# A planned two-layer diffusion step on one core: three conditioning maps go from TensorE to VectorE, and the planner gets a port model and priorities by part

## The chip, the core and the metric

One core of one Trainium2 chip runs the whole kernel. TensorE (PE) multiplies, VectorE (DVE), ScalarE (ACT) and GpSimd (POOL) do the elementwise work, and SyncE (SP) issues every DMA from one queue, in order. The metric is the device time of one execution in microseconds. The kernel before took a median of 1888.9 us in 3 runs (1887.55 to 1890.82).

## The reference, cut to what matters

Two layers work on 384 tokens (128 of context, 256 of a latent grid) of width 1024. Each layer is a half-step FFN, a mixer and a second half-step FFN:

```python
m = (jax.nn.silu(cond) @ lp['ada_w'] + lp['ada_b']).reshape(cond.shape[0], 1, N_MOD, D_MODEL)
x = x + 0.5 * mod(2) * swiglu(modulate(x, lp['norm_w'][0], mod(0), mod(1)), ...)
y, st = mixer(modulate(x, lp['norm_w'][1], mod(3), mod(4)), lp, *mixer_args)
x = x + mod(5) * y
x = x + 0.5 * mod(8) * swiglu(modulate(x, lp['norm_w'][2], mod(6), mod(7)), ...)
```

A conditioning map `(l, m)` is one of the nine slices of `ada_w` of layer `l`: a 1024 x 1024 matrix times two conditioning vectors. Its 4 MB are used once. Maps 1, 4 and 7 scale and 0, 3 and 6 shift the input of the three parts of a layer; 2, 5 and 8 are the gates of their outputs. The mixer projects the input to 23 tiles and runs three sub-mixers on them: an RWKV-7 recurrence, attention, and a gated DeltaNet. Both recurrences are computed in chunks, for which many small triangular matrices are inverted.

## The kernel before, in words

**Products.** Weights are fp32. Each 128-column tile comes by DMA (`wr`), ACT rounds it to fp32r (`whi`), DVE takes the rest (`wlo`), and `mm3` issues three matmuls for each block of 128 rows. An FFN makes 22 pairs of tiles, `pg` and `pu` (24 matmuls each), then 8 tiles `po` (66 matmuls each). DVE and ACT turn a pair into one tile `h`. The norm's factor `rstd` comes from one product `rps`, after the first pairs have been started.

**Conditioning maps.** `SIDE` has one string for each of the six stages (FFN, mixer, FFN of layer 0, the same of layer 1), and its letters give the maps that the stage computes, in the order of `l` and `m` from map 2 of layer 0 on. A letter `v` puts the map on DVE (line 874 on): 8 DMAs of 512 KB (`arow`), and for each two `tensor_tensor_reduce` over 1024 columns against a broadcast vector (`crow`), each followed by a short read of the sum into `mods`. A letter `m` puts it on TensorE: 8 DMAs of 512 KB (`araw`), 16 matmuls of 512 columns into `aps`, a copy `ev`, a way through DRAM (`adas`) and a small product. The kernel before has `"mmm"` for the mixer of layer 0: map 7 and map 8 of layer 0 and map 0 of layer 1.

**Inversion.** `stage_inv` runs twice in a mixer. It inverts 32 x 32 blocks in 31 steps, each of one product `pr` and one subtraction into `Z`, strictly one after the other. Each of the 62 instructions may go to DVE or to POOL.

**What sets the order.** Nothing is issued where it is written. A `Recorder` notes every operation with what it reads and writes, and `order()` plans the whole program: it walks through a modelled time, and each engine takes the waiting operation of the highest priority, which is its longest path to the end plus `BIAS` of its part (`label`). `estimate` gives each operation's planned cost. Where an operation may go to several engines (`op.alts`), the one that would finish it first takes it. On TensorE, `near` says how much less important an operation may be and still go ahead of one that needs another array shape. Where the plan sees TensorE without enough work, it puts in dummy matmuls (`idle_ps`, a 128 x 128 bf16 product that nobody reads), so that the clock stays up; they are fixed instructions of the program. `issue` then emits the plan: nearly all instructions have its line 718, table loads 714 and dummies 706.

Of the kernel before, what the change touches and what calls it, by code (L numbers as in the profile page):

```python
# [33 lines left out]
SHUF = [(j + 16) % 32 for j in range(32)]  # L34


SIDE = ("vvvvv", "mmm", "vvvv", "vvvv", "", "")

ROOM = {"kA": "h", "kS": "h", "vt": "h", "pt": "h", "ev": "h", "w0b": "h", "lora": "h", "yb": "r"}
TUNE = {'near': 2000.0, 'ahead': 8000.0, 'ahead2': 8000.0, 'finish': 5000.0, 'clock': True, 'dummy': 53.5, 'd1': 3600.0, 'd2': 7000.0}  # L40

BIAS = {'ada02': -100000.0, 'ada03': -100000.0, 'ada04': -100000.0, 'ada05': -100000.0, 'ada06': -100000.0, 'ada07': 0.0, 'ada08': 0.0, 'ada10': 0.0, 'ada11': -100000.0, 'ada12': -100000.0, 'ada13': -100000.0, 'ada14': -100000.0, 'ada15': -100000.0, 'ada16': -100000.0, 'ada17': -100000.0, 'ada18': -100000.0}
PLACES = {"u": 30, "r": 3, "w": 6, "a": 3, "b": 2, "h": 5, "t": 10, "ps": 7, "mxs": 2, "dram_ada": 2, "dram_s1": 2, "dram_s2": 2, "dram_s3": 2, "s4": 6}


# [123 lines left out]
class Op:  # L169
    __slots__ = ("eng", "meth", "args", "kw", "cost", "lat", "preds", "succs", "bufs", "idx", "cp", "need", "ready",  # L170
                 "start", "end", "tset", "label", "group", "seed", "filler", "follows", "pos", "held", "stall", "dma", "alts", "done",
                 "name", "real", "parts", "seq", "lead", "mode", "out")


class _Eng:
# [22 lines left out]
class Recorder:  # L198
# [91 lines left out]
    def any(self, *choices):  # L290

        op = self.add(*choices[0][:2], (), choices[0][2])
        op.alts = {}
        for eng, meth, kw in choices:
            op.eng, op.meth, op.kw = eng, meth, kw
            self.estimate(op)
            op.alts[eng] = (meth, kw, op.cost, op.lat, op.tset)
        self.choose(op, min(op.alts, key=lambda e: op.alts[e][2]))
        return op

    def choose(self, op, e):
        op.eng = e
        op.meth, op.kw, op.cost, op.lat, op.tset = op.alts[e]

    def copy(self, out, in_, pool=True):
        c = [("scalar", "copy", dict(out=out, in_=in_)), ("vector", "tensor_copy", dict(out=out, in_=in_))]
# [69 lines left out]
    def estimate(self, op):  # L376
# [4 lines left out]
        views = [v for v in list(a) + list(kw.values()) if isinstance(v, View)]  # L381
        ps = any(v.buf.tag in PSUM for v in views)
        sc = sum(isinstance(kw.get(k), View) for k in ("scalar", "scalar1", "scalar2", "bias", "scale", "accum_out"))
        op.tset, op.dma = None, 0.0
        e, m = op.eng, op.meth
        if m == "dma_start":
            nbytes = n * out.shape[0] * 4
            run = min(v.shape[-1] for v in (out, kw["in_"])) * 4
# [2 lines left out]
        elif e == "tensor":  # L391
            op.lat = 200.0
            op.seq = [self.product(*p) for p in op.parts]
            op.held = sum(p[3] for p in op.seq)
            op.cost = self.stream(0.0, op.seq, [0.0] * 16, 1.0)[1]
            op.mode, op.out = op.seq[0][4], op.seq[-1][4]
        elif e == "vector":
            if m == "tensor_reduce":
                n = int(np.prod(kw["in_"].shape[1:]))
            if m == "reciprocal":  # L400
                n *= 6
            full = ps or m in ("stream_shuffle", "tensor_reduce", "reciprocal") or any(k in kw for k in ("in1", "data"))
            op.cost = (65 + (n if full else n / 2)) / 0.96 + 62 * sc
            if m == "memset":
                op.cost = 8 + n
            op.lat = 130.0
        elif e == "scalar":
            op.cost = ((61 if isinstance(kw["in_"], View) and kw["in_"].buf.tag in PSUM else 112) + n) / 1.2 + 93 * sc
            op.tset = TSETS.get(kw.get("func"))
            op.lat = 142.0  # L410
        else:
            op.cost = 130 + n * (4.3 if sc else 3.3)
            if m == "memset":
                op.cost = 35 + n * 0.83
            elif m == "tensor_tensor":
                op.cost = 150 + n * 2.1
            elif m == "scalar_tensor_tensor":
                op.cost = 95 + n * 1.39
            op.lat = 120.0

    def wait(self, op, o):
        if op.eng == "tensor" and o.eng == "tensor":
# [3 lines left out]
    def order(self):  # L426
# [79 lines left out]
        def enter(op):  # L506
# [4 lines left out]
            else:  # L511
                heapq.heappush(gated, (op.pos - (self.ahead2 if op.follows else self.ahead), op.idx))

        win, busy, over, warm, ndum, past, dens, colt = 0, 0.0, 0.0, False, 0, [], 0.0, [0.0] * 16
        mode, nsw = (P, P), 0
        bus, tset, now, out, emit, wake, stuck = 0.0, None, 0.0, [], [], [], False
        for op in ops:
            if op.need == 0:
                enter(op)
        while len(out) < len(ops):  # L520
# [10 lines left out]
            for e in engs:  # L531
# [6 lines left out]
                while avail[e]:  # L538
# [15 lines left out]
                        op.stall = tag  # L554
                        continue
                    if op.alts:
                        here, best = now + op.alts[e][2], 1e18
                        for f in op.alts:
                            if f != e:
                                queue = sum(ops[x[1]].cost for x in avail[f] if x < item and not ops[x[1]].done)  # L560
                                best = min(best, max(free[f], now) + queue + op.alts[f][2])
# [89 lines left out]
                if op.tset and op.tset != tset:  # L651
                    tset = op.tset
                    cost += 1300.0
                op.start = now
                free[e] = now + cost
                if e != "tensor":
# [1249 lines left out]
```

## Time and profile before

| | us |
|---|---|
| median of 3 runs | 1888.9 |
| the profiled execution | 1892.28 |
| its span, first to last instruction | 1890.5 |
| FFN 1 of layer 0: pairs, then `po` | 184.45 + 92.48 |
| mixer of layer 0 | 360.08 |
| FFN 2 of layer 0 | 191.44 + 92.26 |
| FFN 1 of layer 1 | 191.11 + 92.31 |
| mixer of layer 1 | 349.36 |
| FFN 2 of layer 1 | 189.57 + 92.58 |

The stages were cut where the first matmul of the next one starts in the chain of work that ended last. A mixer includes its output product. Busy times are shown by stage in the section of rows below; in the mixers those of TensorE hold the dummies too, which have rows of their own.

### The profile page before, as it was taken

To read this page: it belongs to the slowest core of one execution; us is meant where nothing else is said; L and a number is where in the kernel's file an instruction comes from. 1 tells how busy PE (TensorE), PEld (TensorE's weight loads), DVE (VectorE), ACT (ScalarE), POOL (GpSimd) and SP (SyncE) were. 2 spreads that over 40 slices of the span, in tenths; PEclk is the share of its full clock that TensorE was granted. 3 is DMA by queue.
4 is the path that set the end of the run, shared out by engine and by line. 5 is a ranking of instruction groups with operands and counts; after the bars stand their busy time and mean duration, and the time that the engine had idled before them with its cause. 6 is when DMAs were issued, how large, how long until landed. Compare 5 with 4: busy or idle time off the path is not lost.

```text
span 1890.5 us, 34461 instructions
## 1 busy us (share of the span) xinstructions
PE 1842.2 (97%) x13589; PEld 1690.1 (89%) x13589; DVE 1336.9 (71%) x2680; ACT 856.4 (45%) x1777; POOL 206.2 (11%) x322
## 2 busy tenths in 40 slices
PE   8999999989999999999999999998899999999998
PEld 6999999778766799999999999997686679999998
DVE  3999954886775679995459995458879646555444
ACT  4444433657445454443344443347664444434323
POOL 0000000251320200000000000014525011000000
PEclk9999999999899999999999999999999999999999
DMA  9566644365421255664455664443341213434442
GB/s 363 200 222 230 241 137 164 124 196 157 109 46 39 78 205 203 216 241 126 125 201 206 214 243 126 126 137 91 79 102 42 66 52 101 123 123 123 128 123 84
DMA packets 144033, 279.46 MB, mean 148 GB/s; under 512 B 50192, under 2 KB 76880, under 8 KB 143872
## 3 DMA queue, kind: packets, MB, share of 16 engines
q1 hardware_dynamic: 143872, 277.26, 46.1%
q8 instruction: 107, 1.75, 0.4%
q14 instruction: 54, 0.44, 0.1%
HBM read 264.80 MB, written 11.89 MB: 146 GB/s over the span
## 4 chain that ended last, share of the span: by engine, by line
PE 82%; DVE 8%; ACT 4%; POOL 2%; DMA 2%; issue 1%; SPq 0%; DVEq 0%; ACTq 0%; POOLq 0%
PE po L718 23%; PE pg L718 20%; PE pu L718 20%; PE pw L718 5%; PE idle_ps L706 3%; POOL pr L718 1%; ACT L714 1%; POOL Z L718 1%; PE q L718 1%; PE z L718 1%; DVE mxs L718 1%; PE gram L718 1%; PE pr L718 1%; PE aps L718 1%; PE sc L718 1%
## 5 line engine op out<-in xcount | busy, mean ns | idle before, releaser
L718 DVE TENSOR_TENSOR wlo<-wr,whi 128x1024 fp32r<-128x1024 f32 (+2 forms) x334 | 400.8, 1203 | 90.4 <-ACT whi L718 90.1
L718 ACT CAST whi<-wr 128x1024 fp32r<-128x1024 f32 (+2 forms) x334 | 339.7, 1019 | 174.4 <-PE po L718 84.4
L718 PE MATMUL pg<-xs,whi 128*128 128x386 f32 x1408 | 366.3, 341 | 0.2 <-POOL xs L718 0.2
L718 PE MATMUL pu<-xs,whi 128*128 128x386 f32 x1408 | 365.8, 341 | 0.0
L718 PE MATMUL po<-h,whi 128*128 128x384 f32 x1408 | 360.1, 337 | 0.0
L718 PEld LDWEIGHTS pg<-xs,whi 128*128 128x128 f32 x1408 | 257.4, 189 | 0.9 <-POOL xs L718 0.5
L718 PEld LDWEIGHTS pu<-xs,whi 128*128 128x128 f32 x1408 | 257.4, 189 | 0.0
L718 DVE CUSTOM_DVE_ANT_0 unread<-arow,crow 128x1024 bf16<-128x1024 f32 x208 | 253.8, 1220 | 3.0 <-ACT crow L718 1.1
L718 PEld LDWEIGHTS po<-h,whi 128*128 128x128 f32 x1408 | 255.7, 188 | 0.0
L718 PE MATMUL pu<-xs,wlo 128*128 128x386 f32 x704 | 238.8, 339 | 0.6 <-DVE wlo L718 0.6
L718 PE MATMUL pg<-xs,wlo 128*128 128x386 f32 x704 | 238.7, 339 | 0.0
L718 PE MATMUL po<-h,wlo 128*128 128x384 f32 x704 | 237.4, 337 | 0.0
L718 PE MATMUL pw<-xs,whi 128*128 128x386 f32 (+1 forms) x736 | 198.4, 350 | 9.8 <-ACT whi L718 7.1
L718 DVE SCALAR_TENSOR_TENSOR xT<-po,mods,xT 128x256 f32<-128x256 f32 (+1 forms) x96 | 35.3, 413 | 169.4 <-PE po L718 169.2
L718 PEld LDWEIGHTS pw<-xs,whi 128*128 128x128 f32 (+1 forms) x736 | 131.7, 186 | 21.3 <-ACT whi L718 8.6
L718 PE MATMUL pw<-xs,wlo 128*128 128x386 f32 (+1 forms) x368 | 128.4, 350 | 7.8 <-DVE wlo L718 7.6
L718 PEld LDWEIGHTS pu<-xs,wlo 128*128 128x128 f32 x704 | 134.1, 190 | 1.1 <-DVE wlo L718 1.1
L718 PEld LDWEIGHTS pg<-xs,wlo 128*128 128x128 f32 x704 | 134.1, 190 | 0.5 <-DVE wlo L718 0.4
L718 PEld LDWEIGHTS po<-h,wlo 128*128 128x128 f32 x704 | 132.1, 188 | 0.0
L706 PEld LDWEIGHTS <-idle_z 128*128 128x128 bf16 x1553 | 96.1, 100 | 33.2 <-issue 26.6
L706 PE MATMUL idle_ps<-idle_z 128*128 128x128 bf16 x1553 | 123.4, 224 | 0.0
L718 ACT CAST h<-up 128x384 fp32r<-128x384 f32 x88 | 45.2, 514 | 151.0 <-DVE up L718 151.0
(363 smaller groups left out, 2466.1 us busy)
## 6 DMA issues: line engine op xcount, KB each, us to landing
wr<-in_ffn_in SPq DMA_DIRECT2D x176, 512.0 KB, 4.5
arow<-in_adat SPq DMA_DIRECT2D x104, 512.0 KB, 3.6
wr<-in_ffn_out SPq DMA_DIRECT2D x64, 512.0 KB, 3.7
wr<-in_w_in SPq DMA_DIRECT2D x44, 512.0 KB, 4.5
wr<-in_ffn_out SPq DMA_DIRECT2D x32, 384.0 KB, 3.3
araw<-in_ada SPq DMA_DIRECT2D x24, 512.0 KB, 5.2
araw<-in_ada SPq DMA_DIRECT2D x32, 256.0 KB, 6.5
wr<-in_w_out SPq DMA_DIRECT2D x16, 512.0 KB, 4.0
```

Of the source, the lines that this page charges most:

```text
L706: self.nc.tensor.matmul(ps[:, 0:n], lhsT=z[:, 0:P], rhs=z, start=True, stop=True)
L714: self.nc.scalar.preload_act_table_set(cur)
L718: ins = getattr(getattr(self.nc, op.eng), meth)(*[fix(x) for x in args], **{k: fix(x) for k, x in kw.items()})
```

## The change

It has four parts. `SIDE` puts the three maps of the first mixer on DVE, so that the six stages compute 6, 0, 5, 4, 0 and 1 maps on DVE instead of 5, 0, 4, 4, 0 and 0, and none on TensorE. The planner gets a model of the SBUF port that DVE and POOL share (`turn`, `op.port`): an operation of one that needs it waits in the plan until the other's is over, and the choice of engine counts that. Some planned costs change, those of POOL mostly upward. `near` goes from 2000 to -1, so that TensorE always takes the operation of the highest priority, and `BIAS` gets 23 entries for parts of the two mixers.

```diff
-SIDE = ("vvvvv", "mmm", "vvvv", "vvvv", "", "")
+SIDE = ("vvvvvv", "", "vvvvv", "vvvv", "", "v")
-TUNE = {'near': 2000.0, 'ahead': 8000.0, ...
+TUNE = {'near': -1.0, 'ahead': 8000.0, ...
+    "attn2.1": 22600.0, "gates.0": 12700.0, "inv0.0": -16400.0, "inv0.1": -22600.0, "inv1.1": -9500.0,
...
-            op.cost = 130 + n * (4.3 if sc else 3.3)
+            op.cost = 480 + n * (4.3 if sc else 3.3)
...
+        if e == "vector" and not ps and m not in ("stream_shuffle", "reciprocal", "tensor_reduce", "memset"):
+            op.port = 2 if src == 2 else 3
+        elif e == "gpsimd":
+            op.port = 1 if m == "memset" else 2
...
+        def turn(e, kind, t):
+            x = port["gpsimd" if e == "vector" else "vector"] if kind else (0.0, 0.0)
+            if kind == 1:
+                return max(t, x[1])
+            return max(t, x[0], x[1] if kind == 3 else 0.0)
...
-                        here, best = now + op.alts[e][2], 1e18
+                        here, best = turn(e, op.alts[e][5], now) + op.alts[e][2], 1e18
...
+                if op.port:
+                    cost += turn(e, op.port, now) - now
```

**TensorE, start of the first mixer.** `pw` is a projection, `aps` a conditioning map, `xs` the scaled input. Before:

```order
L718 MATMUL po_3066<-h_2423,wlo_3124 128x384
L718 MATMUL pw_3174<-xs_2408,whi_3162 128x386 x2
L718 MATMUL aps_3177<-araw_3103,cond_68 32x512 x2
L718 MATMUL aps_3177<-araw_3110,cond_68 32x512 x2
L718 MATMUL pw_3174<-xs_2408,wlo_3170 128x386
L718 MATMUL pw_3174<-xs_2528,whi_3162 128x386 x2
```

and now:

```order
L750 MATMUL po_3107<-h_2422,wlo_3161 128x384
L750 MATMUL pw_3209<-xs_2428,whi_3182 128x386 x2
L750 MATMUL pw_3209<-xs_2428,wlo_3192 128x386
L750 MATMUL pw_3209<-xs_2537,whi_3182 128x386 x2
L750 MATMUL pw_3209<-xs_2537,wlo_3192 128x386
```

The 48 products `aps` of the first mixer (two passes each) and the three small products behind them are gone. The dummies between the mixers' first `pw` and last `po` product go from 552 to 537 in layer 0 and from 595 to 468 in layer 1.

**POOL, second half of the first inversion in the mixer of layer 1.** `R` is the matrix, `pr` and `Z` the two halves of a step, and the size tells the step. Before:

```order
L718 TENSOR_TENSOR pr_13825<-R_13469,Z_13482 112x231
L718 TENSOR_TENSOR Z_13482<-Z_13482,pr_13825 112x21x11
L718 TENSOR_TENSOR pr_13825<-R_13469,Z_13482 112x240
L718 TENSOR_TENSOR Z_13482<-Z_13482,pr_13825 112x20x12
L718 TENSOR_TENSOR pr_13825<-R_13469,Z_13482 112x247
L718 TENSOR_TENSOR Z_13482<-Z_13482,pr_13825 112x19x13
L718 TENSOR_TENSOR pr_13825<-R_13469,Z_13482 112x252
L718 TENSOR_TENSOR pr_13825<-R_13469,Z_13482 112x255
```

and now:

```order
L750 TENSOR_TENSOR pr_13853<-R_13418,Z_13430 112x192
L750 TENSOR_TENSOR Z_13430<-Z_13430,pr_13853 112x24x8
L750 TENSOR_TENSOR Z_13430<-Z_13430,pr_13853 112x22x10
L750 TENSOR_TENSOR pr_13853<-R_13418,Z_13430 112x247
L750 TENSOR_TENSOR Z_13430<-Z_13430,pr_13853 112x18x14
L750 TENSOR_TENSOR Z_13430<-Z_13430,pr_13853 112x17x15
L750 TENSOR_TENSOR pr_13853<-R_13418,Z_13430 112x252
```

Most of the steps that POOL had are on DVE now. Of the 248 instructions `pr` and `Z` of the four inversions POOL had 107 and has 60; DVE goes from 141 to 188.

**DVE, start of the last FFN.** `gt` and `up` are the first work on the pairs, and an `ISA` row is a `tensor_tensor_reduce` of a map, or the read of its sum. Before:

```order
L718 TENSOR_TENSOR wlo_17680<-wr_17644,whi_17670 128x1024
L718 TENSOR_TENSOR wlo_17713<-wr_17676,whi_17703 128x1024
L718 TENSOR_TENSOR wlo_17747<-wr_17709,whi_17733 128x1024
L718 TENSOR_TENSOR gt_17766<-pg_17527,rstd_17743 128x384
L718 TENSOR_TENSOR gt_17771<-pg_17600,rstd_17743 128x384
L718 TENSOR_TENSOR up_17777<-pu_17567,rstd_17743 128x384
```

and now:

```order
L750 ISA unread_17503,mods_15_8193<-arow_17456,crow_17435 128x1024
L750 ISA mods_15_8193 128x1
L750 TENSOR_TENSOR wlo_17562<-wr_17474,whi_17537 128x1024
L750 ISA unread_17503,mods_15_8193<-arow_17456,crow_17442 128x1024
L750 ISA mods_15_8193 128x1
L750 ISA unread_17503,mods_15_8193<-arow_17523,crow_17435 128x1024
L750 ISA mods_15_8193 128x1
L750 TENSOR_TENSOR gt_17607<-pg_17347,rstd_17553 128x384
```

The last FFN now begins with a map, as the two FFNs in the middle did before. The dummies after `rps` go from 42 to 61, from 42 to 54 and from 19 to 54 in the last three FFNs.

## Rows read from the trace of the kernel before

**Rows 1.** The page's busy times of TensorE and its chain by line

```profile
PE 1842.2 (97%) x13589; PEld 1690.1 (89%) x13589; DVE 1336.9 (71%) x2680; ACT 856.4 (45%) x1777; POOL 206.2 (11%) x322
...
PE po L718 23%; PE pg L718 20%; PE pu L718 20%; PE pw L718 5%; PE idle_ps L706 3%; POOL pr L718 1%; ACT L714 1%; POOL Z L718 1%; PE q L718 1%; PE z L718 1%; DVE mxs L718 1%; PE gram L718 1%; PE pr L718 1%; PE aps L718 1%; PE sc L718 1%
```

**Rows 2.** Windows by stage: start:end, length, busy us of each engine, clock, DMA

```profile
41.72:226.17 184.45, 183.82 (x1056) 182.54 (x1056) 175.83 (x297) 81.20 (x157) 0.00 (x0) 1.00 0.66 227
226.17:318.65 92.48, 92.48 (x529) 92.48 (x529) 51.67 (x97) 30.95 (x48) 1.92 (x22) 1.00 0.48 150
318.65:678.73 360.08, 342.82 (x3387) 268.55 (x3387) 261.74 (x655) 195.57 (x458) 90.33 (x120) 0.97 0.39 112
678.73:870.17 191.44, 191.44 (x1102) 190.67 (x1102) 172.92 (x289) 84.66 (x162) 1.30 (x1) 1.00 0.62 214
1245.85:1595.21 349.36, 330.10 (x3329) 267.73 (x3328) 256.32 (x625) 189.68 (x450) 102.38 (x160) 0.98 0.30 80
1595.21:1784.78 189.57, 189.57 (x1079) 189.06 (x1078) 101.37 (x154) 79.93 (x158) 1.30 (x1) 1.00 0.40 122
```

**Rows 3.** Windows of the dummies alone, tile `idle_ps`: length, PE busy, clock, DMA

```profile
318.65:678.73 360.08, 47.87 (x552) 0.97 0.39 112
...
1245.85:1595.21 349.36, 48.41 (x595) 0.98 0.30 80
```

**Rows 4.** Lines of TensorE in the first mixer: busy us, mean ns, idle before

```profile
L718 PE MATMUL aps<-araw,cond 128*32 128x512 f32 x96 | 14.3, 672 | 0.0
```

**Rows 5.** Waits of the DMA queue in the first mixer: us, times, longest

```profile
SPq L718 <- DVE wlo L718: 65.2, 17, 14.2
SPq L718 <- PE aps L718: 62.2, 9, 23.1
```

**Rows 6.** The chain that ended last, 440 to 470 us: start, us, what

```profile
446.98 7.75 DMA wr<-in_w_in
```

**Rows 7.** Timeline of TensorE at the start of the second FFN

```profile
700.58 1.00 PE L706 MATMUL idle_ps<-idle_z 128*128 128x128 bf16 x15
...
701.83 1.68 PE L706 MATMUL idle_ps<-idle_z 128*128 128x128 bf16 x27
```

**Rows 8.** Tile `pr` on POOL in layer 1: ns min/median/max

```profile
L718 POOL TENSOR_TENSOR pr<-R,Z x36: 239/577/2102, 1317.6 to 1460.0; 112x60 f32<-112x60 f32 x4, 112x87 f32<-112x87 f32 x4, 112x31 f32<-112x31 f32 x3, 112x207 f32<-112x207 f32 x3
```

**Rows 9.** Tile `pr` on DVE in layer 0

```profile
L718 DVE TENSOR_TENSOR pr<-R,Z x42: 191/346/1114, 399.6 to 539.9; 112x156 f32<-112x156 f32 x4, 112x192 f32<-112x192 f32 x4, 112x240 f32<-112x240 f32 x4, 112x175 f32<-112x175 f32 x3
```

**Rows 10.** Timeline of POOL, 1330 to 1336 us, in the same inversion

```profile
1331.17 0.60 POOL L718 TENSOR_TENSOR pr<-R,Z 112x220 f32<-112x220 f32 x1
1332.27 2.06 POOL L718 TENSOR_TENSOR pr<-R,Z 112x231 f32<-112x231 f32 x1 [0.50 <-DVE Z L718]
```

**Rows 11.** Timeline of DVE, the same stretch

```profile
1332.64 1.22 DVE L718 TENSOR_TENSOR wlo<-wr,whi 128x1024 fp32r<-128x1024 f32 x1
1333.77 1.89 DVE L718 SCALAR_TENSOR_TENSOR cv<-prj,vecs,cv 128x386 f32<-128x386 f32 x2
```

**Rows 12.** Waits in the mixer of layer 1, 1287 to 1390 us

```profile
DVE Z L718 <- POOL pr L718: 6.8, 4, 2.6
POOL pr L718 <- DVE Z L718: 6.6, 8, 2.7
```

**Rows 13.** Timeline of DVE in the third FFN, with a map beside it

```profile
1030.66 0.55 DVE L718 TENSOR_TENSOR gt<-pg,rstd 128x384 f32<-128x384 f32 x1
1031.13 1.22 DVE L718 TENSOR_TENSOR wlo<-wr,whi 128x1024 fp32r<-128x1024 f32 x1
1032.27 1.22 DVE L718 CUSTOM_DVE_ANT_0 unread<-arow,crow 128x1024 bf16<-128x1024 f32 x1
1033.41 0.08 DVE L718 DVE_READ_ACCUMULATOR2_ANT mods<- 128x1 f32 x1
1033.53 1.22 DVE L718 CUSTOM_DVE_ANT_0 unread<-arow,crow 128x1024 bf16<-128x1024 f32 x1
```

**Rows 14.** Waits of the weight load in the first FFN

```profile
PEld pu L718 <- DVE wlo L718: 1.1, 2, 0.9
```

More of the change, by code (lines that the diff above doesn't have):

```diff
@@ L34 @@
 SHUF = [(j + 16) % 32 for j in range(32)]
-SIDE = ("vvvvv", "mmm", "vvvv", "vvvv", "", "")
+SIDE = ("vvvvvv", "", "vvvvv", "vvvv", "", "v")
 ROOM = {"kA": "h", "kS": "h", "vt": "h", "pt": "h", "ev": "h", "w0b": "h", "lora": "h", "yb": "r"}
-TUNE = {'near': 2000.0, 'ahead': 8000.0, 'ahead2': 8000.0, 'finish': 5000.0, 'clock': True, 'dummy': 53.5, 'd1': 3600.0, 'd2': 7000.0}
-BIAS = {'ada02': -100000.0, 'ada03': -100000.0, 'ada04': -100000.0, 'ada05': -100000.0, 'ada06': -100000.0, 'ada07': 0.0, 'ada08': 0.0, 'ada10': 0.0, 'ada11': -100000.0, 'ada12': -100000.0, 'ada13': -100000.0, 'ada14': -100000.0, 'ada15': -100000.0, 'ada16': -100000.0, 'ada17': -100000.0, 'ada18': -100000.0}
+TUNE = {'near': -1.0, 'ahead': 8000.0, 'ahead2': 8000.0, 'finish': 5000.0, 'clock': True, 'dummy': 53.5, 'd1': 3600.0, 'd2': 7000.0}
+BIAS = {"ada02": -100000.0, "ada03": -100000.0, "ada04": -100000.0, "ada05": -100000.0, "ada06": -100000.0,
[6 rows of a table added]
 PLACES = {"u": 30, "r": 3, "w": 6, "a": 3, "b": 2, "h": 5, "t": 10, "ps": 7, "mxs": 2, "dram_ada": 2, "dram_s1": 2, "dram_s2": 2, "dram_s3": 2, "s4": 6}
@@ L171 @@
                  "start", "end", "tset", "label", "group", "seed", "filler", "follows", "pos", "held", "stall", "dma", "alts", "done",
-                 "name", "real", "parts", "seq", "lead", "mode", "out")
+                 "name", "real", "parts", "seq", "lead", "mode", "out", "port")
 class _Eng:
@@ L296, in any @@
             self.estimate(op)
-            op.alts[eng] = (meth, kw, op.cost, op.lat, op.tset)
+            op.alts[eng] = (meth, kw, op.cost, op.lat, op.tset, op.port)
         self.choose(op, min(op.alts, key=lambda e: op.alts[e][2]))
@@ L302, in choose @@
         op.eng = e
-        op.meth, op.kw, op.cost, op.lat, op.tset = op.alts[e]
+        op.meth, op.kw, op.cost, op.lat, op.tset, op.port = op.alts[e]
     def copy(self, out, in_, pool=True):
@@ L383, in estimate @@
         sc = sum(isinstance(kw.get(k), View) for k in ("scalar", "scalar1", "scalar2", "bias", "scale", "accum_out"))
-        op.tset, op.dma = None, 0.0
+        op.tset, op.dma, op.port = None, 0.0, 0
         e, m = op.eng, op.meth
+        src = sum(isinstance(kw.get(k), View) for k in ("in_", "in0", "in1", "data"))
         if m == "dma_start":
@@ L404, in estimate @@
             if m == "memset":
-                op.cost = 8 + n
+                op.cost = 10 + n * 0.79
+            elif m == "tensor_tensor_reduce":
+                op.cost = 65 / 0.96 + n / 0.96
+            elif not full and out.shape[0] == 112:
+                op.cost = (65 + n) / 0.96
             op.lat = 130.0
@@ L411, in estimate @@
         else:
-            op.cost = 130 + n * (4.3 if sc else 3.3)
+            op.cost = 480 + n * (4.3 if sc else 3.3)
             if m == "memset":
-                op.cost = 35 + n * 0.83
+                op.cost = 50 + n * 0.84
             elif m == "tensor_tensor":
-                op.cost = 150 + n * 2.1
+                op.cost = 165 + n * 2.1 if n > 1 else 450.0
             elif m == "scalar_tensor_tensor":
@@ L516, in order @@
         bus, tset, now, out, emit, wake, stuck = 0.0, None, 0.0, [], [], [], False
+        port = {"vector": [0.0, 0.0], "gpsimd": [0.0, 0.0]}
         for op in ops:
@@ L560, in order @@
                                 queue = sum(ops[x[1]].cost for x in avail[f] if x < item and not ops[x[1]].done)
-                                best = min(best, max(free[f], now) + queue + op.alts[f][2])
+                                best = min(best, turn(f, op.alts[f][5], max(free[f], now)) + queue + op.alts[f][2])
                         if best < here - 60:
@@ L653, in order @@
                     cost += 1300.0
+                if op.port:
+                    cost += turn(e, op.port, now) - now
+                    if op.port == 1:
+                        port[e][1] = now + cost
+                    else:
+                        port[e][0] = now + cost
+                        if op.port == 3:
+                            port[e][1] = now + cost
                 op.start = now
```

5 rows, old and new, of the table BIAS are left out of this document.

## The prediction, made before the changed kernel ran

> **What bounds the kernel now.** I read the page first: TensorE is busy 97% of the span, and the chain that ended last is mostly its own products, `po`, `pg` and `pu` alone 63% [rows 1]. That splits the kernel in two kinds of stages, so the windows by stage came next [rows 2]. In an FFN TensorE is busy to the last microsecond and nothing can be gained but its own products: 191.44 us busy of 191.44 while the pairs are made. There DVE is the neighbour to watch, at 175.83 of 184.45 us in the first FFN. In a mixer the same digit means less. Of 360.08 us in the first mixer TensorE is "busy" for 342.82, but 47.87 of these are 552 dummies, and of 349.36 us in the second one 48.41 are 595 dummies [rows 3]. Dummies and true idle time together are 47.87 + 17.26 = 65.1 us and 48.41 + 19.26 = 67.7 us. So a fifth of each mixer is waiting, and there an order of work can win. Last I looked at what is waited for: the lines and queue waits of the first mixer, then the inversion.
>
> **Maps off TensorE in the first mixer.** The 96 passes `aps` take 14.3 us of TensorE [rows 4]. They also stand in the SP queue: a DMA for the next map waits for `aps` to free a buffer, 62.2 us in 9 waits, the longest 23.1, and every weight and small DMA behind it in that queue waits too [rows 5]. One weight tile then sits on the chain for 7.75 us [rows 6]. The two mixers run the same code on other data, but only the first has maps, so the second is the trace's own answer to "a mixer without maps": 360.08 - 349.36 = 10.7 us. The ends are 0 (the map's products only filled time that dummies fill now) and 14.3 (all of it was on the path). I take 10.7, the twin.
>
> **The new order in both mixers.** A dummy is a fixed instruction, and dropping it gives its time back if the work behind it is ready. Its price: 27 took 1.68 us, 62 ns each, and 15 took 1.00 us, 67 ns each [rows 7]; in the second mixer 48.41 / 595 = 81 ns [rows 3]. I take 70. The second mixer loses 127 dummies (595 to 468): 8.9 us. The first, measured against its twin's 595, has 537, that is 58 fewer: 4.1 us. The ends are 0 (the time comes back as waiting) and 185 x 81 ns = 15.0 us. Setting `near` to -1 could add changes of the array's shape, whose price no row shows alone. Counted over the built order they fall, from 294 to 247 and from 270 to 252, so I add nothing for them.
>
> **The inversion.** Its chain is on the path in places: POOL's `pr` and `Z` are each 1% of the chain that ended last [rows 1]. POOL's median step `pr` is 577 ns, DVE's 346 [rows 8, 9], and 47 of the 248 steps move to DVE. If each were on the path, that is 47 x 0.231 = 10.9 us; it is 0 where the chain has slack. A change of engine costs waits on both sides, 6.8 us of DVE for POOL and 6.6 of POOL for DVE in one inversion [rows 12], but most of TensorE's waiting for it is already in the dummies counted above. I take 3.0, nearer to 0.
>
> What two engines do to each other can be seen beside it. A POOL step of 231 columns took 2.06 us while DVE ran `wlo`, where one of 220 columns took 0.60 just before, and two `cv` on DVE then took 1.89 us together [rows 10, 11]. The Trainium skill (SBUF — State Buffer, Who interferes with whom) says that VectorE with two SBUF inputs and a GpSimd instruction that reads SBUF exclude each other for the whole instruction. The trace agrees here, 2.06 against 0.60. By that rule a plan that knows of it leaves fewer such pairs, and the inversion's term goes to its far end, 10.9 us: the first rival below.
>
> **Maps on DVE in the FFNs.** A map is 16 `tensor_tensor_reduce`. They start 1.26 us apart back to back, and 1.14 us after one the next other work may start [rows 13]: 16 x 1.14 = 18.2 us of DVE each. The first FFN gets a sixth. Its pairs leave DVE only 184.45 - 175.83 = 8.6 us, so some 10 us must lie beside `po`, where 92.48 - 51.67 = 40.8 us are free [rows 2]. In that FFN TensorE waited 1.1 us for `wlo` [rows 14]. I take 0.5 us more, with 0 and 18.2 - 8.6 = 9.6 as the ends. The second FFN gets a fifth: its pairs leave DVE 18.5 us, its `po` more, so 0. The last FFN has the most room (101.37 of 189.57 us): 0 as well. The DMAs only change their place: 8 of 512 KB a map either way, at 227 GB/s and a DMA share of 0.66 at most in the pairs of an FFN [rows 2].
>
> **The start of the FFNs.** After `rps` TensorE waits for `rstd`, DVE and ACT, and the order fills the wait with dummies: 42 of them between 700.58 and 703.51 us, with two passes of `pu` among them [rows 7]. In the new order the runs are 61, 54 and 54 instead of 42, 42 and 19, because a map now stands ahead of `gt` in the last FFN and more stands there in the others. That is 66 more, at 70 ns 4.6 us lost. The ends are 0 (TensorE would have waited anyway) and 66 x 81 ns = 5.3. Nine small products of the states (5 `btk`, 4 `sd`) also move from the first mixer's end into the second FFN's pairs. Most lie in or near this wait and cost nothing; at a dummy's 81 ns they would cost 0.7 us, which the mixer would have paid before.
>
> **The sum.** -10.7 - 4.1 - 8.9 - 3.0 + 0.5 + 4.6 = -21.6 us. On the profiled execution that is 1892.28 - 21.6 = 1870.7 (its span 1890.5 and 1.8 around it). The median of the runs lies 3.4 us below the profiled one, so I predict 1867.3.
>
> **Rivals.**
> Further down: the maps were wholly on the path and the two engines stop blocking each other. -14.3 - 15.0 - 10.9 + 5.1 = -35.1, or 1853.8. For it: the 62.2 us of queue waits, the 2.06 us step. Against it: mixers have other chains (tables, projections, recurrence) that stay.
>
> The dropped dummies come back as waiting. They are where the plan saw no work, and before the change the trace has 17.26 and 19.26 us of idle time that the plan did not fill either. Then -10.7 + 5.1 = -5.6, or 1883.3. For it: a plan tuned in its own model looks best there. Against it: that plan now counts waits it did not count.
>
> An FFN becomes DVE's: what doesn't fit beside the first FFN's pairs delays each `wlo`. That is 9.6 us instead of 0.5, -12.5 in all, or 1876.4. For it: DVE at 95% of that stretch. Against it: 40.8 free microseconds beside `po`, and the order puts reductions there.
>
> Slower: DVE becomes the bound of the mixers. It takes 47 steps of 346 ns from POOL, 16.3 us, and 12 additions `sqacc` besides (0.47 us of DVE each, an estimate from the step from `gt` to the next start, 1030.66 to 1031.13 [rows 13]), 5.6 us: 21.9 us on an engine that was busy 261.74 of 360.08 us. If all of it lands ahead of a `wlo` or `pg` that TensorE waits for, and the dummies come back too, the sum is -5.6 + 21.9 = +16.3, or 1905.2. It decides once more than 5.6 / 21.9, a quarter, lands so and the dropped dummies have bought nothing. For it: no weight tile is multiplied before DVE has made its `wlo`. Against it: 98 us of the first mixer are without DVE work.
>
> **How the numbers follow.** The forecast gets 0.50, its own range is 1859 to 1877. Further down 0.17, dummies back as waiting 0.18, the FFN 0.07, slower 0.08. The range from 1851 to 1884 leaves out the slower case and the outer half of the first rival's spread. A difference under 0.2% (3.8 us) is about what runs of this kernel can't tell from none, so faster means under 1885.1: all of the forecast but 0.01, the rival below, the FFN case, and half of the case at 1883.3, 0.49 + 0.17 + 0.07 + 0.09 = 0.82. The other half of that case gives most of 0.09 for the same, and 0.09 is left for slower.
>
> **What would show it.** The first mixer should be about 344 us and the second about 339, with 537 and 468 dummies, and no SP wait for `aps`. The pairs of the second, third and last FFN should take 1 to 3 us longer, with all DVE waits of TensorE there under 2 us. It is wrong if the second mixer stays near 349 with more idle time (dummies back as waiting), if `po` of the first FFN grows past 95 us, or if TensorE's waits for `wlo` and `pg` in the mixers double.

## The result, and the profile after

The changed kernel took a median of 1837.06 us in 4 runs (1833.19 to 1841.44), the one before 1889.86 beside it: a ratio of 0.9722 (95% interval 0.9693 to 0.9752). The difference is -52.8 us. The prediction had the sign, and with 1867.3 us (-21.6) less than half of the size. The time is also below the range.

The page of the kernel after, busy times and chain by line, to be read against [rows 1]:

```profile
PE 1807.8 (98%) x13421; PEld 1681.1 (91%) x13421; DVE 1374.3 (75%) x2806; ACT 867.3 (47%) x1819; POOL 134.6 (7%) x248
...
PE po L750 24%; PE pg L750 11%; PE pu L750 11%; PE pw L750 8%; DVE unread L750 7%; DVE wlo L750 5%; PE idle_ps L738 3%; DVE up L750 2%; DMA wr<-in_ffn_in 1%; PE q L750 1%; PE z L750 1%; PE gram L750 1%; PE dd L750 1%; PE w L750 1%; DVE gt L750 1%
```

`pr` and `Z` of POOL, 1% each of the chain before, are not among its lines any more, and 12% of the chain now runs through DVE's maps (`unread`) and remainders (`wlo`). POOL lost a third of its busy time. The windows by stage (start:end, length, busy us of each engine, clock, DMA share, GB/s) say where the time came from, in the order first FFN, its `po`, first mixer, second FFN, third FFN, second mixer, last FFN:

```profile
42.06:227.60 185.54, 183.81 (x1059) 182.14 (x1059) 179.78 (x304) 80.49 (x157) 0.00 (x0) 1.00 0.65 232
227.60:320.17 92.57, 92.57 (x530) 92.57 (x529) 66.14 (x125) 33.19 (x52) 0.69 (x14) 1.00 0.55 182
320.17:642.77 322.60, 315.29 (x3258) 262.10 (x3257) 255.05 (x652) 195.72 (x466) 61.62 (x104) 0.98 0.32 86
642.77:837.78 195.01, 193.56 (x1137) 191.50 (x1136) 183.79 (x312) 86.93 (x168) 0.00 (x0) 1.00 0.65 227
930.53:1122.98 192.45, 191.47 (x1115) 189.94 (x1114) 172.10 (x289) 83.86 (x161) 0.00 (x0) 1.00 0.62 211
1215.30:1540.76 325.46, 318.96 (x3202) 264.06 (x3201) 247.75 (x645) 190.89 (x469) 68.78 (x108) 0.96 0.33 86
1540.76:1731.65 190.89, 190.89 (x1114) 190.15 (x1113) 119.15 (x189) 84.61 (x162) 0.00 (x0) 1.00 0.47 149
```

The mixers give 37.5 and 23.9 us, the four rows of FFN pairs take 7.3 back. `po` of the first FFN, which now has reductions beside it, stays at 92.57. The same windows for the dummies alone, in the two mixers:

```profile
320.17:642.77 322.60, 40.87 (x537) 0.98 0.32 86
1215.30:1540.76 325.46, 38.05 (x468) 0.96 0.33 86
```

A mixer's length is TensorE's real work, its dummies and its true idle time (length less busy). With [rows 2, 3] on the left:

| us | mixer 0 before | after | mixer 1 before | after |
|---|---|---|---|---|
| real work | 294.95 | 274.42 | 281.69 | 280.91 |
| dummies | 47.87 (552) | 40.87 (537) | 48.41 (595) | 38.05 (468) |
| idle | 17.26 | 7.31 | 19.26 | 6.50 |
| length | 360.08 | 322.60 | 349.36 | 325.46 |

The idle time fell by 10.0 and 12.8 us; no term of the forecast had it. Dummies and idle time together fell by 17.0 and 23.1 us, where the forecast had 4.1 and 8.9. In the first mixer the real work fell by 20.5, of which 14.3 are `aps` [rows 4]. It also ran at a lower clock for less time: a mean of 0.97 over 360.08 us against 0.98 over 322.60 lacks 10.8 and 6.5 us of full clock, some 4 us between them as far as means of two digits tell. The second mixer's mean clock went the other way, 0.98 to 0.96, and it is faster all the same.

The queue waits of SP in the first mixer after (us in total, times, longest), for [rows 5]:

```profile
SPq L750 <- DVE wlo L750: 57.8, 16, 6.7
SPq L750 <- DVE L L750: 52.8, 5, 26.7
SPq L750 <- DVE Z L750: 46.0, 5, 20.2
```

Nothing waits for `aps`; in its place stand `L` and `Z`, data of the recurrences. At the start of the second FFN, TensorE's timeline (start, us, what) shows the longer fill that was predicted, 61 dummies where [rows 7] had 42:

```profile
665.03 1.67 PE L738 MATMUL idle_ps<-idle_z 128*128 128x128 bf16 x27
666.58 0.33 PE L750 MATMUL btk<-cst,bt 128*128 128x128 f32 x1
666.75 0.27 PE L750 MATMUL btk<-cst,kt 128*128 128x128 f32 x1
666.86 2.06 PE L738 MATMUL idle_ps<-idle_z 128*128 128x128 bf16 x34
```

And POOL's half-steps `pr`, layer 0 and layer 1 (ns min/median/max), for [rows 8]:

```profile
L750 POOL TENSOR_TENSOR pr<-R,Z x17: 285/547/892, 406.2 to 527.0; 112x192 f32<-112x192 f32 x4, 112x175 f32<-112x175 f32 x2, 112x231 f32<-112x231 f32 x2, 112x207 f32<-112x207 f32 x2
L750 POOL TENSOR_TENSOR pr<-R,Z x17: 237/549/1960, 1285.2 to 1430.3; 112x60 f32<-112x60 f32 x3, 112x135 f32<-112x135 f32 x2, 112x156 f32<-112x156 f32 x2, 112x192 f32<-112x192 f32 x2
```

In the first layer the longest `pr` on POOL took 2287 ns before and takes 892; in the second, where the step of [rows 10] lay, one of 1960 ns is left. The median of that layer hardly moved, 577 to 549 ns: what changed is mostly the tail, and `Z` still has steps of 1455 and 1538 ns.

### The profile page after: what moved, and what is told of

Same layout as the page of the kernel before. It is cut to its first block, busy times and chain, and to the rows that moved or that the text cites. A ratio compares the mean times of both kernels' runs of the same rounds, so it can differ in the third digit from the quotient of the medians.

```text
span 1838.4 us, 34124 instructions
## 1 busy us (share of the span) xinstructions
PE 1807.8 (98%) x13421; PEld 1681.1 (91%) x13421; DVE 1374.3 (75%) x2806; ACT 867.3 (47%) x1819; POOL 134.6 (7%) x248
## 4 chain that ended last, share of the span: by engine, by line
PE 69%; DVE 19%; DMA 5%; issue 4%; ACT 3%; SPq 0%; POOL 0%; DVEq 0%; ACTq 0%; POOLq 0%
PE po L750 24%; PE pg L750 11%; PE pu L750 11%; PE pw L750 8%; DVE unread L750 7%; DVE wlo L750 5%; PE idle_ps L738 3%; DVE up L750 2%; DMA wr<-in_ffn_in 1%; PE q L750 1%; PE z L750 1%; PE gram L750 1%; PE dd L750 1%; PE w L750 1%; DVE gt L750 1%
## 5 line engine op out<-in xcount | busy, mean ns | idle before, releaser
L750 DVE TENSOR_TENSOR wlo<-wr,whi 128x1024 fp32r<-128x1024 f32 (+1 forms) x334 | 397.4, 1192 | 70.8 <-ACT whi L750 70.6
L750 DVE CUSTOM_DVE_ANT_0 unread<-arow,crow 128x1024 bf16<-128x1024 f32 x256 | 312.1, 1219 | 5.9 <-ACT crow L750 2.9
L738 PE MATMUL idle_ps<-idle_z 128*128 128x128 bf16 x1487 | 110.9, 222 | 0.0
L738 PEld LDWEIGHTS <-idle_z 128*128 128x128 bf16 x1487 | 89.0, 99 | 21.4 <-issue 14.9
```

The lines of the kernel that those rows point to most:

```text
L738: self.nc.tensor.matmul(ps[:, 0:n], lhsT=z[:, 0:P], rhs=z, start=True, stop=True)
L750: ins = getattr(getattr(self.nc, op.eng), meth)(*[fix(x) for x in args], **{k: fix(x) for k, x in kw.items()})
```

## The experiments

The four parts of the change were put in one by one, then taken out one by one; then the cause underneath was tried by itself. Mixers are given as length, dummies and idle time of the first and the second. The kernel before, run beside each, stayed between 1889 and 1891 us. The letters in the expectations name theories, each with what it expects beside it; what follows says which of them a run bore out.

**The new `SIDE` alone, in the kernel before.**

```diff
-SIDE = ("vvvvv", "mmm", "vvvv", "vvvv", "", "")
+SIDE = ("vvvvvv", "", "vvvvv", "vvvv", "", "v")
```

> The planner of before, with only the new SIDE: all maps on VectorE. The first mixer has no maps, and 566 dummies in each mixer. Theory P (the extra gain is the priorities by part): the maps alone are worth what the prediction took, the first mixer comes to about 349 us, like the second, the FFNs lose about 4 us: 1882 us, about 7 below before. Theory Q (the port model is what counts): the same here. Theory M (moving the maps was worth far more than 10.7 us, through the DMA queue): first mixer near 335 us, 1868 us or less.

Measured: 1876.11 us, ratio 0.9934 (0.9918 to 0.9951). The first mixer fell to 347.18, the second to 345.91. All engines and then the dummies alone, first and second mixer:

```profile
318.01:665.19 347.18, 325.38 (x3300) 264.84 (x3299) 256.69 (x621) 191.04 (x454) 101.73 (x160) 0.98 0.30 80
1231.13:1577.04 345.91, 327.45 (x3300) 267.03 (x3299) 257.40 (x621) 191.02 (x454) 102.12 (x160) 0.98 0.31 81
318.01:665.19 347.18, 45.76 (x566) 0.98 0.30 80
1231.13:1577.04 345.91, 45.85 (x566) 0.98 0.31 81
```

Moving the maps is worth 13 us in all: the first mixer gives 12.9 and becomes like its twin, the second gives 3.5, and the FFNs take some 3 back. P and Q, which say the same here, come nearest, with 7 us and a mixer of 349; M, with 335, falls. Idle time is 21.8 and 18.5 us: it does not come from the maps.

**With the port model and the planned costs added, no priorities, `near` as before** (the edit is against the kernel after).

```diff
-TUNE = {'near': -1.0, ...
+TUNE = {'near': 2000.0, ...
-    "attn2.1": 22600.0, "gates.0": 12700.0, "inv0.0": -16400.0, ...
```

> New SIDE, the port model and the new costs, but near 2000 and no priorities by part. 800 and 788 dummies in the mixers, 56 of the 248 inversion steps on POOL. Theory Q (port): most of the gain is here already, mixers under 335 us, 1850 us or less, with POOL and VectorE seldom stretched. Theory P (priorities): 1875 to 1890 us, mixers 345 us or more, in spite of the port model; the true idle time of TensorE in a mixer falls from 17 to 19 us to under 10, and dummies take its place.

Measured: 1878.95 us, 0.9955 (0.9939 to 0.997), 2.8 us more than without the model, which the two intervals do not tell from none.

```profile
320.23:666.00 345.77, 336.56 (x3534) 276.19 (x3533) 253.87 (x646) 196.96 (x470) 62.65 (x106) 1.00 0.31 81
1237.62:1579.90 342.28, 333.24 (x3522) 274.87 (x3521) 252.91 (x645) 198.16 (x472) 64.55 (x105) 1.00 0.31 82
320.23:666.00 345.77, 59.95 (x800) 1.00 0.31 81
1237.62:1579.90 342.28, 58.77 (x788) 1.00 0.31 82
```

This is the row that the prediction lacked. Idle time is 9.2 and 9.0 us, less than half, and dummies rose from 566 to 800 and 788. The plan now sees the waits that it didn't see, and fills them; it also leaves POOL less to do, 62.65 us instead of 101.73. By itself that gains nothing, as P had it: a wait has only changed its name.

**The same with `near` at -1** (the kernel after without its 23 priorities).

```diff
-    "attn2.1": 22600.0, "gates.0": 12700.0, "inv0.0": -16400.0, ...
```

> The changed kernel without the 23 priorities by part (near -1, port model, new costs, new SIDE stay). 736 dummies in each mixer. Theory P: it loses most of what the prediction had not foreseen, 1865 to 1880 us, each mixer 12 us or more longer than in the changed kernel. Theory Q: within 8 us of the changed kernel, 1845 us or less.

Measured: 1865.31 us, 0.9879 (0.9864 to 0.9894); mixers 336.42 (736 dummies, 7.34 idle) and 337.33 (736, 8.38). So `near` gains 13.6 us without priorities, where the prediction had nothing for it, and the priorities bring the last 28.2, as P had it and not Q.

**All as after, but no port in the plan.**

```diff
-            op.port = 2 if src == 2 else 3
+            op.port = 0
...
-            op.port = 1 if m == "memset" else 2
+            op.port = 0
```

> The changed kernel with the port left out of the plan; priorities, costs, near and SIDE stay. 104 inversion steps on POOL again, 721 and 567 dummies in the mixers. Theory Q: the time goes back to 1870 us or more, and stretched POOL and VectorE instructions come back to about 23 us each in a mixer. Theory P has two readings: if the priorities help any plan, it stays under 1855 us; if they fit only the plan that they were made for, it also goes back, to 1865 us or more.

Measured: 1893.68 us, 1.0021 (1.001 to 1.0033), with all priorities and `near` -1.

```profile
321.36:674.57 353.21, 335.53 (x3455) 276.40 (x3454) 263.15 (x632) 194.76 (x467) 87.16 (x139) 0.98 0.29 79
1246.93:1594.91 347.98, 330.61 (x3301) 268.61 (x3300) 257.79 (x629) 187.82 (x456) 99.42 (x149) 0.98 0.30 80
```

Idle time is back at 17.7 and 17.4 us (353.21 - 335.53, 347.98 - 330.61), and the whole gain is gone: Q, and the second reading of P. The stretched instructions are back as well, with 23.9 and 27.2 us on DVE and 21.6 and 23.7 on POOL in the two mixers (how this is counted stands under the inversion below). These priorities need the model that they were made under. Priorities made for a plan without the port, with POOL's work left in place, were not run, so it is not shown that such a plan could gain nothing.

**The 23 values dealt to the parts at random.**

```diff
-    "attn2.1": 22600.0, "gates.0": 12700.0, "inv0.0": -16400.0, "inv0.1": -22600.0, ...
+    "attn2.1": 5700.0, "gates.0": -21400.0, "inv0.0": -11900.0, "inv0.1": -11300.0, ...
```

> The changed kernel with the same 23 values of the priorities, dealt out to the 23 parts in another, random order. 852 and 746 dummies in the mixers. Theory P1 (the values fit this plan): it is slower than the kernel without them (1865.3 us), by the dummies about 1873 us, with true idle time still under 10 us a mixer since the plan knows the port. Theory P2 (any shake of the priorities helps): 1855 us or less.

Measured: 1874.88 us, 0.9914 (0.9899 to 0.9929); mixers 343.17 (852, 5.63) and 338.54 (746, 6.68). That is 9.6 us slower than no priorities at all, on the side of P1. One deal was run; it shows that the assignment matters, not how lucky a deal can be.

**As after, with `near` at 2000.**

```diff
-TUNE = {'near': -1.0, ...
+TUNE = {'near': 2000.0, ...
```

> The changed kernel with near back at 2000, the rest as changed. 741 and 696 dummies in the mixers. Without priorities, near at -1 gained 13.6 us. Theory P1: the priorities fit only the plan that they were found in, so this one loses most of their 28 us too: 1865 to 1875 us, idle time under 10 us a mixer. Theory N (near is a gain of its own, which adds to the others): 1837 + 14, about 1851 us.

Measured: 1859.55 us, 0.9835 (0.982 to 0.9849); mixers 338.77 (741, 10.06) and 332.83 (696, 5.66). It loses 22.5 us, more than the 13.6 that `near` gains by itself: the priorities were fitted to that rule. The time is between those of P1 and N, nearer to P1's.

**As after, with the planned costs of before.**

```diff
-            op.cost = 480 + n * (4.3 if sc else 3.3)
+            op.cost = 130 + n * (4.3 if sc else 3.3)
...
-                op.cost = 165 + n * 2.1 if n > 1 else 450.0
+                op.cost = 150 + n * 2.1
```

> The changed kernel with the planned costs of before, the port model, near, SIDE and priorities as changed. 844 and 585 dummies, 58 inversion steps on POOL. Theory P1: the priorities no longer fit, 1865 to 1885 us, with idle time near 8 us since the port is in the plan. Theory C (small wrong costs don't matter): within 8 us of the changed kernel.

Measured: 1859.08 us, 0.9831 (0.9815 to 0.9848); mixers 346.77 (844, 8.20) and 329.80 (585, 7.28). Idle time stays low, so the port model does without the costs; the priorities don't. Most of the loss is in the first mixer, with 307 dummies more. C, which had 1845 us or less, falls; P1's 1865 is not reached.

**As after, with the maps back on TensorE** (`SIDE` of before).

```diff
-SIDE = ("vvvvvv", "", "vvvvv", "vvvv", "", "v")
+SIDE = ("vvvvv", "mmm", "vvvv", "vvvv", "", "")
```

> The changed kernel with the SIDE of before: three maps on TensorE in the first mixer. 662 dummies there, and the second mixer has 468 as in the changed kernel. With the planner of before the maps cost 13 us. If the terms add, 1850 us, all of it in the first mixer, and the second stays at 325.5 us. If the priorities fit only their plan, the first mixer goes to 350 us or more and the total to 1860 to 1866 us, the second mixer still at 325.5.

Measured: 1870.96 us (1860.83 to 1872.98), 0.9884 (0.9856 to 0.9912); mixers 355.04 (662, 10.43) and 324.75 (468, 5.92). The second mixer has its 468 dummies and its time as after. The first loses 32 us, 125 dummies and the maps' own products, more than the 13 that the maps are worth alone. The mixers are as the second reading had them, 350 us or more and 325.5, and the total is 5 us above its range.

**No additions, products or copies on POOL; the plan knows of no port** (the kernel before with the new `SIDE`, and POOL only fills tiles).

```diff
         c = [("scalar", "copy", ...), ("vector", "tensor_copy", ...)]
-        if pool and in_.buf.tag not in PSUM:
-            c.append(("gpsimd", "tensor_copy", dict(out=out, in_=in_)))
...
-        return self.any(("vector", "tensor_tensor", kw), ("gpsimd", "tensor_tensor", kw))
+        return self.vector.tensor_tensor(**kw)
```

> The planner of before, which knows no port, with the new SIDE, but POOL may only fill with constants: every addition, product and copy that it had goes to VectorE or ScalarE, so that nothing reads SBUF on POOL beside VectorE. 605 dummies in each mixer. Theory K (the 17 to 22 us of idle time a mixer that no plan of this kind filled are collisions of POOL and VectorE): idle time falls to 6 to 9 us, a mixer to 295.7 us + 57.8 ns for each dummy, 331 us, and the total from 1876.1 us (new SIDE alone) to about 1845 us, without port model and priorities. Theory L (idle time comes from the planner's wrong costs or from VectorE's load): idle stays at 17 us or more, and with 39 more dummies a mixer and 20 us more of work on VectorE it takes 1880 us or more.

Measured: 1854.39 us, 0.9823 (0.9805 to 0.9841), with the old order, old `near` and no priorities.

```profile
317.16:652.01 334.85, 325.55 (x3339) 267.48 (x3338) 256.92 (x716) 192.64 (x467) 15.73 (x34) 0.98 0.31 83
1218.92:1555.62 336.70, 327.24 (x3339) 268.75 (x3338) 257.20 (x716) 192.92 (x467) 15.71 (x34) 0.98 0.31 83
317.16:652.01 334.85, 49.00 (x605) 0.98 0.31 83
1218.92:1555.62 336.70, 49.28 (x605) 0.98 0.31 83
```

Against the first experiment, DVE has 716 instructions in the first mixer instead of 621, and is busy for 256.92 us instead of 256.69. The 95 more cost it nothing, since its own are shorter now, such as `cv` in the first mixer, first with POOL's arithmetic and then without:

```profile
L718 DVE SCALAR_TENSOR_TENSOR cv<-prj,vecs,cv 128x386 f32<-128x386 f32 x24 | 17.3, 729 | 0.3
L716 DVE SCALAR_TENSOR_TENSOR cv<-prj,vecs,cv 128x386 f32<-128x386 f32 x24 | 14.6, 608 | 0.0
```

Idle time fell from 21.8 and 18.5 to 9.3 and 9.5. The 39 dummies more fill part of that, 3.2 us in the first mixer, and yet the mixers are 12.3 and 9.2 us shorter. POOL's planned costs, which go out together with its work, do not explain it: with the new costs and no port in the plan the idle time was 17.7 and 17.4, with the old costs and the port 8.2 and 7.3. So about half of the time that the old plan did not fill was POOL and DVE holding each other up. That is K's mechanism, and L falls. The mixers are 4.2 and 6.0 us longer than K had them for these 605 dummies, and the total is 9 us above K's; where that went was not found.

**All 248 half-steps of the inversion on DVE, then on POOL** (as after otherwise; `nc.gpsimd` in the second).

```diff
-                nc.tt(p3, ..., ALU.mult)
-                nc.tt(Z[:, 0:c, c:32], Z[:, 0:c, c:32], p3, ALU.subtract)
+                nc.vector.tensor_tensor(out=p3, ..., op=ALU.mult)
+                nc.vector.tensor_tensor(out=Z[:, 0:c, c:32], ..., op=ALU.subtract)
```

> The changed kernel with all 248 inversion steps on VectorE, the rest as changed, planned anew: 720 and 626 dummies. Theory Y (with the port in the plan, a mixer's length follows its dummies, about 298 us + 58 ns for each, whatever set the order): mixers of 339.5 and 334 us, 1862 us in all. Theory I (the inversion's engine is what counts, since a step takes 346 ns there against 577): 1837 us or less, mixers as in the changed kernel or shorter.

> The changed kernel with all 248 inversion steps on POOL, planned anew: 887 and 737 dummies. Theory Y: mixers of 349 and 341 us, 1879 us in all. Theory I: 188 more steps on POOL at 231 ns more each, 43 us, so 1880 us, and the idle time of TensorE in the mixers grows to 15 us or more since waits for POOL lie on its path.

Measured: on DVE 1865.95 us, 0.9867 (0.9848 to 0.9886), mixers 340.21 (720, 7.99) and 333.77 (626, 6.15); on POOL 1882.78 us, 0.996 (0.9923 to 0.9997), mixers 348.36 (887, 8.71) and 340.88 (737, 6.74). All engines in the first mixer, on DVE and on POOL:

```profile
321.29:661.50 340.21, 332.22 (x3454) 274.90 (x3453) 254.36 (x668) 196.34 (x473) 54.13 (x87) 0.98 0.32 82
```

```profile
320.71:669.07 348.36, 339.65 (x3621) 282.67 (x3620) 236.02 (x540) 199.15 (x479) 126.68 (x207) 0.99 0.31 80
```

and the 62 `pr` of that mixer:

```profile
L750 DVE TENSOR_TENSOR pr<-R,Z 112x31 f32<-112x31 f32 (+15 forms) x62 | 21.1, 340 | 3.2 <-DMA R<-s 2.7
L750 POOL TENSOR_TENSOR pr<-R,Z 112x31 f32<-112x31 f32 (+15 forms) x62 | 38.6, 623 | 17.4 <-DVE wlo L750 10.9 <-DMA R<-s 2.1
```

Idle time is low in both, though POOL is busy for 126.68 us in one: where a plan knows of the conflict, the engine of the steps does not decide the idle time. It does decide how many dummies the plan puts in, 887 against 720, and with them some 17 us of the total. On DVE that is Y and against I, which had 1837 us or less; on POOL both had the time (1879 and 1880), and only the idle time, 15 us or more by I, speaks against I. The lengths follow the dummies, as Y expected. Over 13 mixers of the other port-aware plans above with no map on TensorE (both of the kernel after, of the two runs without priorities, of the random deal, of `near` at 2000 and of the old costs, and the second one where the maps are back), the lengths lie on a line of 295.7 us and 57.8 ns for each dummy, with a scatter of 2.3 us; these four lie 1.4 to 2.9 us above it. The mixers of plans that don't know the port, with POOL's arithmetic in them and no map on TensorE (the second one before, and both of `SIDE` alone and of no port), lie 16 to 20 us above the same line.

**Three maps of the second FFN pushed back** (as after, against the 3.6 us that its pairs lost).

```diff
+    "ada07": -100000.0, "ada08": -100000.0, "ada10": -100000.0,
```

> The changed kernel with maps 7 and 8 of layer 0 and 0 of layer 1 at the low priority of the other maps. The mixers keep their 537 and 468 dummies, the second FFN has 60 after its start instead of 64. Theory L (maps of high priority in the second FFN stand ahead of wlo and cost it the 1.5 us of idle time that its pairs show): 1835.5 us, the pairs of that FFN at 193.5 us or less instead of 195.0. Theory S (TensorE waits there for rstd and not for maps): 1837 us, no difference.

Measured: 1842.93 us, 0.9745 (0.9723 to 0.9767), no gain: the number of S and not of L. The pairs of the second FFN took 195.38 us with 1.45 idle, as after. But that idle time is no wait for `rstd` either: most of it stands before products with `wlo`. Other runs tell what it goes with. The pairs of the second FFN with `SIDE` alone, with the costs of before, and with the maps back on TensorE:

```profile
665.19:856.45 191.26, 191.21 (x1105) 190.10 (x1104) 179.16 (x300) 84.01 (x161) 1.31 (x1) 1.00 0.64 225
664.68:856.83 192.15, 191.61 (x1105) 189.88 (x1104) 178.82 (x301) 83.75 (x161) 0.00 (x0) 1.00 0.65 224
674.72:868.56 193.84, 192.53 (x1118) 190.76 (x1117) 172.29 (x290) 85.30 (x162) 0.00 (x0) 1.00 0.62 212
```

The first two plan with the old costs and have the same five maps on DVE: 0.05 and 0.54 us idle. The third has the new costs and one map less: 1.31. Without the port it is 1.96, without priorities 1.75. So the waits come with the new planned costs, and not with the fifth map, the port or the priorities.

**More priorities, and priorities without POOL's help.** The first replaces the table by one of 49 entries made for a shorter plan, 33 of them for parts of the mixers instead of 23, and pushes the three maps back as in the run before; the second leaves POOL the fills alone, as above, with the planner of after and 50 entries made for that, 37 for the mixers. The edit is that of the first.

```diff
-    "attn2.1": 22600.0, "inv1.1": -9500.0, "scD0.1": -11900.0, "scD1.1": -3000.0, ...
+    "attn2.1": 24700.0, "inv1.1": -21000.0, "scD0.1": -6100.0, "scD1.1": 23900.0, "unit.0": 11700.0, ...
+    "ada07": -100000.0, "ada08": -100000.0, "ada10": -100000.0, ...
```

> The changed kernel with other priorities, more of them (49 entries in all), chosen because the plan with the port comes out shorter; POOL may take the same work. 486 and 448 dummies in the mixers, 20 fewer at the starts of the FFNs. Theory Y (295.7 us + 57.8 ns a dummy, idle under 10 us): mixers of 323.8 and 321.6 us, together some 3 us less than in the changed kernel, and 1 us in the FFNs: 1832 to 1834 us. Theory F (the plan is at its end, what is gained in it is lost on the chip): 1837 us or more, with idle time of 10 us or more in a mixer.

> The changed planner, POOL only filling with constants, and priorities made for that plan. 506 and 395 dummies. Theory Y with what the kernel without reads on POOL showed (4.1 to 6.0 us a mixer above that line): mixers of 325 to 331 and 318.5 to 324.5 us, so 1834 to 1843 us. Theory Z (without POOL's reads nothing collides, so a plan needs no port model and priorities fit better): mixers on the line or below, 1831 us or less.

Measured: 1828.48 us in 5 runs (1825.25 to 1831.23), 0.9674 (0.9659 to 0.9689), and 1832.43 us, 0.9698 (0.9681 to 0.9715). The two mixers with all of POOL's work:

```profile
319.88:639.54 319.66, 310.27 (x3220) 257.34 (x3219) 250.64 (x629) 200.61 (x484) 69.22 (x115) 0.99 0.33 87
1211.04:1524.71 313.67, 309.20 (x3152) 256.84 (x3151) 250.07 (x640) 193.67 (x464) 65.94 (x112) 0.98 0.33 88
319.88:639.54 319.66, 36.25 (x486) 0.99 0.33 87
1211.04:1524.71 313.67, 34.25 (x448) 0.98 0.33 88
```

and with POOL only filling:

```profile
319.81:643.87 324.06, 312.53 (x3240) 260.28 (x3239) 263.01 (x725) 193.44 (x462) 12.23 (x33) 0.99 0.33 86
1217.20:1531.50 314.30, 308.34 (x3129) 255.07 (x3128) 259.34 (x721) 189.45 (x465) 12.68 (x31) 0.99 0.32 89
```

The first beats both kernels, 8.6 us below the one after, and F falls. The second is within 4 us of it, which the two intervals hardly tell apart, with POOL nearly idle, 12 us busy in a mixer: POOL's arithmetic buys almost nothing here. Its mixers lie 0.9 and 4.2 us below the line, as Z had it, and its time lies between those of Z and Y. The second mixer of the first lies 8 us below the line, so the line is no law outside the plans that made it.

## Why the prediction was wrong, and what of it held

**What the gain is made of.** From 1889 us: the maps -13.0, port model and costs +2.8, `near` -13.6, priorities -28.2. The steps were measured in this order, and others would share it out differently: taken out of the finished kernel, the maps cost 33.9 us, the port 56.6, `near` 22.5 and the priorities 28.2. Each was part of what the priorities were fitted to.

**Maps off TensorE: right.** The twin gave 10.7 us; alone they were worth 12.9 in that mixer, inside its ends. The waits for `aps` are gone, as predicted.

**The new order in both mixers: this step failed.** Its term was -13.0 us, with the inversion's -16.0; once the maps were off, the mixers fell by 24.6 and 20.5 us, 45.0 together (347.18 to 322.60, 345.91 to 325.46). It went wrong in two ways. The 17.26 and 19.26 us of idle time were shown in the sum of what a mixer wastes, and then left standing: no term let them fall, and they fell by 22.7 us together. Nor can that be added by itself, since filling the waits alone gained nothing. And dummies were compared between two plans as if they meant the same. The plan of before did not see 17 to 19 us of a mixer's waiting, so it had fewer dummies than a plan of that length needs. The 537 and 468 have to be set against the 800 and 788 of the same rules with the port in the plan: 263 and 320 fewer, at 57.8 ns 15.2 and 18.5 us, where the prediction had 58 and 127. Measured between these two kernels are 23.2 and 16.8 us. The price of a dummy, 70 ns, was too high, and that mattered less than the count.

**`near` at nothing: wrong.** The changes of the array's shape were counted and fell, and so were put at no cost. But the rule also decides which product comes first: the dummies fall from 800 and 788 to 736 and the mixers by 9.4 and 5.0 us, with TensorE's real work nearly the same in the first (276.61 and 276.60). At 57.8 ns the dummies make up 3.7 and 3.0 us of that. Changes of shape, counted in the two traces, fell too, from 280 and 274 to 240 and 240, and may be part of the rest; their price is not shown. They don't decide: with the priorities and `near` at 2000 the first mixer has 234 of them against 247 after, and is 16.2 us longer.

**The inversion: left open in size.** The term was 3.0 us for 47 steps at a shorter duration. The 231 ns set POOL's steps of one layer against DVE's of the other, in different sizes; over the same 62 `pr` the difference is 283 ns (340 and 623). Moved wholly to one engine, its cost follows the plan's dummies, so it can't be told from the order. The far end of 10.9 was laid to fewer stretched steps in the inversion alone. The stretching was everywhere: summed over all instructions of a mixer, by what each took above the tenth percentile of its operation and shape in the whole trace, where that is over 60 ns (a count of my own from the traces), DVE had 21.9 and 26.2 us of it before and has 16.8 and 12.7, POOL 22.7 and 24.7 before and 10.3 and 11.5. With the old planner and the new `SIDE` DVE has 27.3 and 28.3, and 7.3 and 7.4 once POOL only fills. Not all of it lies on the path.

**The FFNs: nearly right, somewhat low.** The terms were +0.5 and +4.6; the pairs took 1.1, 3.6, 1.3 and 1.3 us more. The dummies after `rps` were as counted. In the second FFN, TensorE's weight loads waited for `wlo` four times, 2.4 us in all and 1.0 at the longest; that is the part that was put at nothing. It goes with the new planned costs, for which the forecast had no term: with the old ones and the same five maps the pairs took 191.26 and 192.15 us instead of 195.01, and the idle time was 0.05 and 0.54 instead of 1.45.

**The rivals.** The first had the mechanism, engines that stop blocking each other, and was priced too low at -35.1 us, since it too left the idle time in place. The second, dropped dummies that come back as waiting, is the opposite of what happened: dummies and waiting fell together. But the case against it, that the plan now counts waits it did not count, was the point, and it should have been carried into the sum. DVE did not become the bound of a mixer: it is busy 255.05 and 247.75 us there, less than before. The third, an FFN that becomes DVE's, did not come either: the first FFN's pairs took 1.1 us more where 9.6 were feared, its `po` stayed at 92.57, and the second's waits go with the costs.

By the Trainium skill (SBUF — State Buffer, Who interferes with whom), a DVE instruction with two SBUF inputs excludes a GpSimd instruction that reads SBUF, not one that only writes it. The trace agrees: with only fills left on POOL, DVE did 95 instructions more in the same 256.9 us, and its stretched time fell from 27.3 to 7.3 us.

## What to carry to other kernels

True idle time in a stage that a plan thinks full shows that the plan does not know something; ask first whether the change teaches it that. Fillers can be compared only between plans with the same knowledge, and a model that knows of a conflict gained nothing here until an order was made under it. Before scheduling around a conflict between two engines, try taking the weaker one's share away: here that gave 21.7 us of 1876 with the old order.

## What the runs showed of the hardware

- POOL's help to DVE is of almost no use here: without POOL's arithmetic DVE runs 95 instructions more in the same busy time (256.69 and 256.92 us), and 12.5 and 9.0 us of TensorE's idle time are gone.
- The same 62 products `pr` took a mean of 340 ns on DVE and 623 ns on POOL.
- Between the 13 mixers of the line, a dummy less went with 57.8 ns less of a mixer's length, while those that ran were busy for 76 to 81 ns each in the mixers after (40.87 / 537 and 38.05 / 468).
- The mean granted clock does not decide a mixer: the second one after has a lower mean than before, 0.96 against 0.98, and is 23.9 us faster.
